# Two plain f blocks per layer instead of three, and an earlier, closer placing of the norm and the token sums in the feed-forward stage

## The chip, the cores and the metric

The kernel runs on one core of one Trainium2 chip. The metric is device time in microseconds (us) of one execution; a smaller number is better. On the core, TensorE (PE) does matmuls into PSUM, VectorE (DVE) and ScalarE (ACT) do elementwise work, GpSimd (POOL) helps in other stages, and SyncE (SP) issues the DMAs.

## The reference, cut to what matters

Two decoder layers of width 1024 on 528 tokens (16 meta tokens and 512 real ones). Each layer is a mixing part and a feed-forward part; the change touches only the second.

```python
hn = rmsnorm(h, ffn_norm_g)
ff = jax.nn.silu(jnp.einsum('bld,df->blf', hn, w_gate)) * jnp.einsum('bld,df->blf', hn, w_up)
return h + jnp.einsum('blf,fd->bld', ff, w_down)          # d = 1024, f = 2816
```

The tensors are float32. The kernel gets that precision from reduced-precision matmuls by splitting each operand into a high and a low part and adding three products: high by high, high weight by low data, low weight by high data.

## The kernel before, in words

The state `h` lies transposed, as eight tiles of 128 rows (k = 0 to 7) by 528 tokens. A layer's feed-forward stage goes over f in 22 blocks of 128 rows, grouped in the six rounds of `ROUNDS` (3, 4, 4, 4, 4, 3 blocks). While the gate and up products of one round run, the down products of the round before are placed between them.

An f block is done in one of two ways.

- A *plain* block (f below `PLAIN`) is two calls of `dense_steps`, one for gate and one for up. Each has 8 steps, one for each k. In layer 0 a step is 6 matmuls of 264 columns (three products, two halves of the tokens); in layer 1, where only the 512 real tokens are wanted, a step is 3 matmuls of 512 columns. So a plain block is 96 matmuls of 264 columns or 48 of 512, recorded at line 217. Its weights are split in pieces of 128x512 by ACT (high part, line 191) and DVE (low part, `wlo`, line 194).
- A `Unit` does gate and up together by a scheme of seven half-size products in place of eight (a Winograd form of a 2 by 2 block product: two weight halves by two halves of the tokens). That is 7 x 4 x 3 = 84 matmuls of 264 columns, or of 256 in layer 1 (line 880). Three of the products take plain halves of the tokens, `xh`/`xl`; the other four take *token sums*, the tiles `th`/`tl`, which `x_forms(0)` to `x_forms(3)` build once per layer: on ACT a scaling (line 841) and a high split (line 142), on DVE four sums of 264 columns (lines 842, 844, 845) and a low split of 1056 columns (line 143). The weights have sums too: `make1` to `make4` build the four weight operands w1 to w4, DVE with four additions (lines 914, 915, 921, 927) and low splits of up to 128x1024 at line 869, ACT with the high splits at line 868. A unit's PE work is in three parts: `head` (24 matmuls, plain token halves, w1), `middle` (36 matmuls; the first of them take w2 and the token sums) and `tail` (24 matmuls). If no down product waits to be placed, a unit's tail stands behind the next unit's head.

Ahead of all this, `start_ffn` scales and splits `h` into `xh` and `xl`. `squares` sums the squares of `h`, and `rstd` turns them into the norm's factor `R`: two matmuls against ones per half (line 290), then a Newton step on DVE (lines 297, 299, 300). `g_done(0)`, the first gate block's evaluation, is held back until `R` exists.

PE's order is the program's order exactly (`tc.manual_schedule`). The other engines' orders are chosen by the scheduler when the kernel is built, and are then fixed: each engine takes its instructions one behind the other and waits on semaphores. Weight loads are issued by SP as soon as a buffer of the ring (`raw`, three deep; `fraw`, two deep) is free.

Of the kernel before, what the change touches and what calls it, by code (L numbers as in the profile page):

```python
# [16 lines left out]
NK = D // 128  # L17
# [7 lines left out]
DFF = 2816  # L25
NF = DFF // 128
ROUNDS = ((0, 3), (3, 7), (7, 11), (11, 15), (15, 19), (19, 22))
PLAIN = 3
HB = NK // 2
EPS = 1e-6  # L30
NBLK = SEQ // 128
# [8 lines left out]
def hybrid_kernel(ctx, tc, x_t, w_in, w_fl, w_out, w_gate, w_up, w_down, vecs, b_fg, rope, decay, mask, ident, out_t):  # L40
# [81 lines left out]
    def sv(t, real, p0=0, p1=128):  # L122
        if real:
            return t[p0:p1, META:T]
        return t[p0:p1, 0:T].rearrange("p (a b) -> p a b", a=2)

    def pv(ps, real, p0=0, p1=128):
        if real:
            return ps[p0:p1, 0, 0:SEQ]
        return ps[p0:p1, :, 0:HALF]  # L130
# [6 lines left out]
    def vcol(c):  # L137
        return vec[:, c:c + 1]


    def split(hi, lo, src, pinned=False):
        pin(nc.scalar.copy(hi, src), pinned)
        pin(nc.vector.tensor_sub(lo, src, hi.bitcast(F32)), pinned)
# [102 lines left out]
    def merge(base, *placed):  # L246

        todo = sorted((p for group in placed for p in group), key=lambda p: p[0])
        out = []
        for i, f in enumerate(base):  # L250
            while todo and todo[0][0] <= i:
                out.append(todo.pop(0)[1])
            out.append(f)
        return out + [f for _, f in todo]
# [11 lines left out]
    def tt(name, dt=F32):  # L266
        tag, bufs = tags[name]
        return tmp.tile([128, T], dt, name=name, tag=tag, bufs=bufs)
# [4 lines left out]
    def fft(tag, dt=F32R, shape=(128, T), bufs=None):  # L273
        return phase["ffn"].tile(list(shape), dt, name=tag, tag=tag, bufs=bufs)

    def col_parts(src, cols, pinned=False):
        c_all = slice(cols[0][0], cols[-1][1])
        sh = tt("sqh", F32R)
        sl = tt("sql", F32R)
        split(sh[:, c_all], sl[:, c_all], src[:, c_all], pinned)  # L280
        return sh, sl

    def col_rstd(parts, n, cols, rname):


        c_all = slice(cols[0][0], cols[-1][1])
        views = [psum_a()[:, 0:c1 - c0] for c0, c1 in cols]
        for i, s in enumerate(parts):
            for v, (c0, c1) in zip(views, cols):
                nc.tensor.matmul(v, ones if s.dtype == F32R else ones.bitcast(F32), s[:, c0:c1], start=(i == 0), stop=(i == len(parts) - 1))  # L290
        with tc.high_priority():
            r = tt(rname)
            a = tt("nwt")
            for v, (c0, c1) in zip(views, cols):
                nc.scalar.activation(r[:, c0:c1], v, AF.Ln, bias=epsc, scale=1.0 / n)
            nc.scalar.activation(r[:, c_all], r[:, c_all], AF.Exp, scale=-0.5)
            nc.vector.tensor_mul(a[:, c_all], r[:, c_all], r[:, c_all])
            for v, (c0, c1) in zip(views, cols):
                nc.vector.scalar_tensor_tensor(a[:, c0:c1], v, n * EPS, a[:, c0:c1], ALU.add, ALU.mult)
            nc.vector.scalar_tensor_tensor(r[:, c_all], a[:, c_all], 3.0 * n, r[:, c_all], ALU.subtract, ALU.mult)  # L300
        return r
# [24 lines left out]
    def squares(st, cols, pinned=False, att=True):  # L326
        c = slice(cols[0][0], cols[-1][1])
        acc = tt("ss")
        for k in range(NK):
            if k == 0:  # L330
                first = nc.scalar.activation(acc[:, c], h[0][:, c], AF.Square)
                if pinned:
                    tc.keep_in_program_order(first)
            else:
                sq = tt("sq")
                more = nc.scalar.activation(sq[:, c], h[k][:, c], AF.Square)
                if pinned:
                    tc.keep_in_program_order(more)
                with ExitStack() if att else tc.high_priority():
                    nc.vector.tensor_add(acc[:, c], acc[:, c], sq[:, c])  # L340
        if pinned:
            st["acc"] = acc
            return
        with ExitStack() if att else tc.high_priority():
            st["parts"] = col_parts(acc, cols)

    def rstd(st, cols, rname="R"):

        st["R"] = col_rstd(st["parts"], D, cols, rname)
# [56 lines left out]
    def silu(t, then=None):  # L406
        nc.scalar.activation(t, t, AF.Silu)
        if then:
            tc.keep_in_program_order(nc.scalar.preload_act_table_set(then))
# [383 lines left out]
    def ffn(l, st, real, last):  # L793
        QC = REAL if real else FULL
# [5 lines left out]
        held = []  # L800

        def two(t):
            return t[:, t0:T].rearrange("p (a b) -> p a b", a=2)
# [4 lines left out]
        def g_done(f):  # L808
            def go(ps):
                sg = tt("sg")  # L810
                if isinstance(ps, list):
                    for v, (c0, c1) in zip(ps, QC):
                        nc.vector.scalar_tensor_tensor(sg[:, c0:c1], v[:, 0:c1 - c0], RSC, st["R"][:, c0:c1],
                                                       ALU.mult, ALU.mult)
                else:
                    nc.vector.scalar_tensor_tensor(sv(sg, real), pv(ps, real), RSC, sv(st["R"], real), ALU.mult, ALU.mult)
                silu(sv(sg, real))
                sgs[f] = sg
            return go
# [14 lines left out]
        def x_forms(k):  # L834
            def go():
                if k == 0:
                    st["t"] = [[fft(f"t{p}{i}", shape=(128, 2, 4, w)) for p in "hl"] for i in range(2)]
                s = fft("S", F32, (128, 6, w), 2)
                a, b = ((h[k][:, c0:c1], h[HB + k][:, c0:c1]) for c0, c1 in HC)
                g0, g1 = vcol(V_FFN + l * NK + k), vcol(V_FFN + l * NK + HB + k)  # L840
                nc.scalar.activation(s[:, 0:2], two(h[k]), AF.Copy, scale=g0)
                nc.vector.tensor_sub(s[:, 2], s[:, 1], s[:, 0])
                for i in range(2):
                    nc.vector.scalar_tensor_tensor(s[:, 3 + i], b[1], g1, s[:, 1 + i], ALU.mult, ALU.subtract)
                nc.vector.scalar_tensor_tensor(s[:, 5], a[1], g1, s[:, 4], ALU.mult, ALU.subtract)
                th, tl = (t[:, k % 2] for t in st["t"][k // 2])
                split(th, tl, s[:, 2:6])
            return go
# [177 lines left out]
        steps = []  # L1026
        tails = []
        fills = []
        for r, (f0, f1) in enumerate(ROUNDS):
            for f in range(f0, f1):  # L1030
                if f < PLAIN:
                    steps += dense_steps(w_gate[l, f], [(0, xs, NK, QC, g_done(f) if f else held.append)], banks=f == 1)
# [10 lines left out]
                if fills:  # L1043
                    p, g0, g1 = fills.pop(0)
# [18 lines left out]
        else:  # L1063
# [149 lines left out]
            places = [(end, after_a)] + [(end + n * (i + 1), f) for i, f in enumerate(  # L1213
                (after_0, after_1, after_2, after_3, after_4, after_5, after_6, after_7))]
            steps += merge(rnd, places)
        for i in range(HB):
            steps.insert(NK + 4 + 9 * i, x_forms(i))
        steps.insert(NK + 4, lambda: g_done(0)(held[0]))
        steps.insert(NK + 4, lambda: rstd(st, QC))
        steps.insert(4, lambda: squares(st, QC, False, False))  # L1220
        return steps

    gf = const.tile([128, NK], F32, name="gf")
    nc.vector.tensor_scalar_mul(gf, vec[:, V_FIN:V_FIN + NK], RSC)
# [1 line left out]
    def layer(l):  # L1226
# [79 lines left out]
        for g in range(2):  # L1306
# [15 lines left out]
                      ret_places(3, 52, 45.5, 47.5, 57.5, 55.5, 58.5, 60, 64.1, 63, 64.2))  # L1322
        plan += [op[3], op[7], op[11], op[15]] + op[16:]
        up = ffn(l, ff, real, real)
        plan += [lambda: enter("ffn"), start_ffn] + up
        return plan
# [78 lines left out]
```

## Time and profile before

| | us |
|---|---|
| median of 3 runs | 1274.46 |
| range of those runs | 1274.37 to 1275.15 |
| the profiled execution, its own time | 1278.19 |
| span of that execution in the trace | 1276.3 |
| feed-forward stage of layer 0 begins (first plain matmul) | about 290 |
| feed-forward stage of layer 1 begins | about 918 |
| granted PE clock, mean over the span | 0.995 |

The profiled execution is 3.7 us over the median of the runs. A page's first block gives each engine's busy time. The chain of waits follows the work that ended last; where it names PE with nothing between, PE never waited there. A row of a timeline gives start, duration, engine, line, operation and, in brackets, idle time ahead of it. A row of the stretches gives a stretch's length, each engine's busy time in it, the granted PE clock and the share of the DMA engines. Two instructions on DVE overlap by some 0.08 us in these records, so the distance from one start to the next is what one costs.

### The profile page before, as it was taken

The page shows a single profiled execution, that of the slowest core. Times are in us where ns is not written, and L with a number is a line of the kernel's source. Part 1 is how long each engine was busy: PE and PEld are TensorE (multiplying, and loading weights), DVE is VectorE, ACT ScalarE, POOL GpSimd, SP SyncE. Part 2 cuts the span into 40 slices and gives each one's busy share as a digit, 9 for nine tenths or more (in the row PEclk, how much of TensorE's full clock was granted, in tenths as well). Part 3 has the DMA queues.
Part 4 walks back from the last instruction along what each step waited for, and adds up shares of the span by engine and source line. Part 5 has one row for each costly group of instructions (what it writes and reads, how often), then busy time and mean ns, then how long its engine had stood idle before and what let it go on. Part 6 is the DMA issues. An engine that isn't in the chain of part 4 may idle for free.

```text
span 1276.3 us, 23615 instructions
## 1 busy us (share of the span) xinstructions
PE 1258.8 (99%) x9271; PEld 1199.9 (94%) x9271; DVE 996.6 (78%) x1843; ACT 688.2 (54%) x1246; POOL 265.2 (21%) x522
## 2 busy tenths in 40 slices
PE   9999999999999999999999999999999999999997
PEld 8899999999999999999998989999789999999996
DVE  7777856779988887887785777567899888888866
ACT  6666545676444444444464665456764444444444
POOL 3355546420000000000025545554100000000000
PEclk9999999999999999999999999999999999999998
DMA  6322232223333333332323232232224333333321
GB/s 216 93 68 84 79 94 72 74 67 112 108 96 100 100 100 100 100 100 83 102 74 100 76 100 84 75 92 67 99 86 129 100 100 100 100 99 101 106 76 67
DMA packets 45680, 120.57 MB, mean 94 GB/s; under 512 B 5360, under 2 KB 12272, under 8 KB 45568
## 3 DMA queue, kind: packets, MB, share of 16 engines
q1 hardware_dynamic: 45136, 118.77, 29.8%
q8 instruction: 73, 1.20, 0.4%
q14 instruction: 39, 0.32, 0.1%
q10 hardware_dynamic: 432, 0.29, 0.1%
HBM read 116.91 MB, written 2.13 MB: 93 GB/s over the span
## 4 chain that ended last, share of the span: by engine, by line
PE 94%; DVE 2%; ACT 1%; DMA 1%; issue 0%; DVEq 0%; ACTq 0%; SPq 0%
PE psd L217 30%; PE psa L880 18%; PE psd L1015 14%; PE psd L880 13%; PE psa L217 5%; PE psa L1015 4%; PE psa L418 2%; PE psa L572 2%; PE psa L507 2%; PE psa L729 1%; PE psa L699 1%; DMA bc<-cdr 1%; PE psa L379 1%; PE psa L290 0%; DMA cdr<-z 0%
## 5 line engine op out<-in xcount | busy, mean ns | idle before, releaser
L194 POOL TENSOR_TENSOR wlo<-raw,whi 128x128 fp32r<-128x128 f32 x504 | 259.9, 551 | 293.5 <-ACT whi L191 293.5
L217 PE MATMUL psd<-xh,whi 128*128 128x264 f32 (+1 forms) x792 | 197.1, 316 | 0.6 <-ACT whi L191 0.6
L217 PE MATMUL psd<-xh,wlo 128*128 128x264 f32 (+1 forms) x792 | 187.7, 305 | 0.0
L217 PE MATMUL psd<-xl,whi 128*128 128x264 f32 (+1 forms) x792 | 187.3, 304 | 0.4 <-DVE xl L320 0.4
L217 PEld LDWEIGHTS psd<-xh,whi 128*128 128x128 f32 x792 | 129.4, 191 | 5.7 <-ACT whi L191 1.3
L217 PEld LDWEIGHTS psd<-xh,wlo 128*128 128x128 f32 x792 | 128.0, 190 | 6.4 <-DVE wlo L194 0.4
L217 PEld LDWEIGHTS psd<-xl,whi 128*128 128x128 f32 x792 | 128.6, 190 | 4.8 <-DVE xl L320 0.8
L191 ACT CAST whi<-raw 128x512 fp32r<-128x512 f32 (+1 forms) x168 | 98.5, 614 | 51.6 <-PE psd L217 38.2
L868 ACT CAST whi<-raw 128x1024 fp32r<-128x1024 f32 (+2 forms) x62 | 54.9, 886 | 51.0 <-PE psd L880 39.5
L868 ACT CAST fwhi<-raw 128x1024 fp32r<-128x1024 f32 (+2 forms) x62 | 55.7, 898 | 46.6 <-PE psd L880 39.2
L1115 POOL TENSOR_TENSOR th<-th,e 128x544 f32<-128x544 f32 x1 | 1.4, 1370 | 359.1 <-DVE e L1135 359.1
L85 POOL MEMSET kl<- 64x528 f32 x2 | 1.1, 534 | 345.4 <-PE psa L880 345.4
L869 DVE TENSOR_TENSOR wlo<-raw,whi 128x1024 fp32r<-128x1024 f32 (+2 forms) x62 | 62.9, 1015 | 12.1 <-ACT whi L868 12.0
L869 DVE TENSOR_TENSOR fwlo<-raw,fwhi 128x1024 fp32r<-128x1024 f32 (+2 forms) x62 | 64.0, 1032 | 9.6 <-ACT fwhi L868 9.5
L880 PE MATMUL psa<-th,whi 128*128 128x264 f32 (+1 forms) x232 | 65.4, 282 | 0.0
L880 PE MATMUL psa<-th,wlo 128*128 128x264 f32 (+1 forms) x232 | 65.4, 282 | 0.0
L880 PE MATMUL psa<-tl,whi 128*128 128x264 f32 (+1 forms) x232 | 65.3, 282 | 0.0
L880 PE MATMUL psa<-th,fwhi 128*128 128x264 f32 (+1 forms) x224 | 63.4, 283 | 0.0
L880 PE MATMUL psa<-tl,fwhi 128*128 128x264 f32 (+1 forms) x224 | 63.3, 283 | 0.0
L880 PE MATMUL psa<-th,fwlo 128*128 128x264 f32 (+1 forms) x224 | 63.2, 282 | 0.0
L527 ACT ACTIVATE probs<-probs,nmax 128x144 f32<-128x144 f32 (+1 forms) x64 | 36.9, 577 | 47.3 <-DVE nmax L514 34.5
L868 ACT CAST fwhi<-S 128x1024 fp32r<-128x1024 f32 x20 | 21.0, 1050 | 69.1 <-PE psa L880 67.1
(340 smaller groups left out, 4053.7 us busy)
## 6 DMA issues: line engine op xcount, KB each, us to landing
raw<-w_in SPq DMA_DIRECT2D x54, 512.0 KB, 3.5
raw<-w_gate SPq DMA_DIRECT2D x44, 512.0 KB, 3.8
fraw<-w_up SPq DMA_DIRECT2D x38, 512.0 KB, 3.5
raw<-w_down SPq DMA_DIRECT2D x64, 256.0 KB, 2.8
raw<-w_out SPq DMA_DIRECT2D x16, 512.0 KB, 3.4
raw<-w_down SPq DMA_DIRECT2D x32, 192.0 KB, 2.5
bc<-cdr SPq DMA_DIRECT2D x16, 264.0 KB, 3.4
raw<-w_up SPq DMA_DIRECT2D x6, 512.0 KB, 3.6
```

What stands on the lines that cost most here:

```text
L191: pin(nc.scalar.copy(hi, job["raw"][:, c0:c1]), pinned)
L194: pin(sub(lo[:, i:i + step], job["raw"][:, c0 + i:c0 + i + step], hi[:, i:i + step].bitcast(F32)), pinned)
L217: nc.tensor.matmul(ps[1][b][:, 0:c1 - c0], w[:, wk, :], x[:, c0:c1], start=(k == 0 and i == 0), stop=(k == n - 1 and i == 2))
L379: nc.tensor.matmul(ps[:, 0:c1 - c0], wf[:, k, :], st["x"][k][part][:, c0:c1], start=(i == 0), stop=(i == 2 * NK - 1))
L418: nc.tensor.transpose(ps[:, 128 * j:128 * j + 128], src[:, o:o + 128], idt)
L507: nc.tensor.matmul(sc[0:nq, 0:c1 - c0], st["q"][s][:, q0:q0 + nq], kk[:, c0:c1], start=(i == 0), stop=(i == 1))
L527: nc.scalar.activation(pr, pr, AF.Exp, bias=nmax[0:nq], scale=-1.0, accum_out=rsum)
L572: nc.tensor.matmul(po[:, c0:SEQ], v[:, j, :], pp[:, j, META + c0:T], start=(j == 0 and i == 0), stop=(j == 4 and i == 1))
L868: nc.scalar.copy(hi, src)
L869: nc.vector.tensor_sub(lo, src, hi.bitcast(F32))
L880: nc.tensor.matmul(bank()[:, 0:b.shape[-1]], a[:, o + k, :], b, start=(fresh and k == 0 and i == 0), stop=(k == n - 1 and i == 2), skip_gr ...
L1015: nc.tensor.matmul(v[:, 0:c1 - c0], a[:, s * n + k, :], b[:, c0:c1], start=(k == 0 and i == 0), stop=(k == n - 1 and i == 2))
```

## The change

`PLAIN` goes from 3 to 2, so f = 2 becomes the first unit of its layer; each layer then has 2 plain blocks and 20 units instead of 3 and 19. The rounds stay. Since round 0 has no down products to place, the tail of unit 2 comes behind the head of unit 3.

The list of places is rewritten with `merge`. Counted in the plain steps, `squares` stays ahead of step 4; `rstd`, `g_done(0)` and `x_forms(0)` move from ahead of step 12 to ahead of step 11; `x_forms(1)` to `(3)` move from ahead of steps 20, 28 and 36 to ahead of steps 16, 21 and 26. There were 48 plain steps before the first unit's head, and there are 32 now.

```diff
-PLAIN = 3
+PLAIN = 2
...
-        for i in range(HB):
-            steps.insert(NK + 4 + 9 * i, x_forms(i))
-        steps.insert(NK + 4, lambda: g_done(0)(held[0]))
-        steps.insert(NK + 4, lambda: rstd(st, QC))
-        steps.insert(4, lambda: squares(st, QC, False, False))
-        return steps
+        return merge(steps, [(4, lambda: squares(st, QC, False, False)), (NK + 3, lambda: rstd(st, QC)),
+                             (NK + 3, lambda: g_done(0)(held[0]))], [(p, x_forms(i)) for i, p in enumerate((11, 16, 21, 26))])
```

PE, layer 0, the up product of f = 0: the difference of the two orders (- before, + now). `sqh` and `sql` are the split sum of squares, `ones` the matrix that sums it.

```order
 L217 MATMUL psd<-xl_4147,whi 128x264 x2
 L217 MATMUL psd<-xh_4146,wlo 128x264 x2
+L290 MATMUL psa<-sqh,ones 128x264 x2
+L290 MATMUL psa<-sql,ones 128x264 x2
 L217 MATMUL psd<-xh_4150,whi 128x264 x2
 L217 MATMUL psd<-xl_4151,whi 128x264 x2
 L217 MATMUL psd<-xh_4150,wlo 128x264 x2
-L290 MATMUL psa<-sqh,ones 128x264 x2
-L290 MATMUL psa<-sql,ones 128x264 x2
 L217 MATMUL psd<-xh_4154,whi 128x264 x2
```

The norm's products moved ahead by one step, six matmuls.

DVE, layer 0, the rows that end with the low split of w2, the first operand that a unit's middle needs. Before the change this is unit 3, behind the three plain blocks:

```order
L825 TENSOR_TENSOR tq<-tq,sg 128x528
L845 SCALAR_TENSOR_TENSOR S<-h_80,vec,S 128x264
L194 TENSOR_TENSOR wlo<-raw,whi 128x512
L143 TENSOR_TENSOR al_4487<-tq,ah_4486 128x528
L914 TENSOR_TENSOR S<-fraw 128x512
L143 TENSOR_TENSOR tl_4306<-S,th_4305 128x1056
L816 SCALAR_TENSOR_TENSOR sg<-psd,R 128x528
L869 TENSOR_TENSOR wlo<-raw,whi 128x1024
L915 TENSOR_TENSOR S<-S,raw 128x512
L921 TENSOR_TENSOR fraw<-raw,fraw 128x512
L927 TENSOR_TENSOR raw<-raw,S 128x512
L869 TENSOR_TENSOR fwlo<-S,fwhi 128x1024
```

The same place with the change, where it is unit 2, behind two plain blocks:

```order
L824 SCALAR_TENSOR_TENSOR tq<-psd,R 128x528
L845 SCALAR_TENSOR_TENSOR S<-h_80,vec,S 128x264
L825 TENSOR_TENSOR tq<-tq,sg 128x528
L914 TENSOR_TENSOR S<-fraw 128x512
L143 TENSOR_TENSOR tl_4300<-S,th_4299 128x1056
L143 TENSOR_TENSOR al_4495<-tq,ah_4494 128x528
L915 TENSOR_TENSOR S<-S,raw 128x512
L921 TENSOR_TENSOR fraw<-raw,fraw 128x512
L927 TENSOR_TENSOR raw<-raw,S 128x512
L869 TENSOR_TENSOR fwlo<-S,fwhi 128x1024
```

The plain split at line 194 and the gate evaluation at line 816, which belong to the third plain block, are gone from this piece; the split of w1 (`wlo<-raw`, 128x1024) stands further up. All the rest is still there. Counted from the low split of the squares (`sql<-ss`, line 143) to this `fwlo<-S` and both included, layer 0 has 51 DVE instructions before the change and 46 with it, layer 1 49 and 44. In both layers the five that are gone are four splits at line 194 and one evaluation at line 816.

## The prediction

> **What bounds the kernel now.** I read the page's busy times first, then who waited for whom, then the two feed-forward openings engine by engine.
>
> ```profile
> PE 1258.8 (99%) x9271; PEld 1199.9 (94%) x9271; DVE 996.6 (78%) x1843; ACT 688.2 (54%) x1246; POOL 265.2 (21%) x522
> ```
>
> PE is the bound: a matmul taken away is worth its time, and a wait put in costs its time. The list of waits says how little PE waits; its longest wait is not in the stage that changes.
>
> ```profile
> PE psa L418 <- DVE vv L484: 1.8, 1, 1.8
> ...
> PE psd L217 <- DVE xl L320: 0.4, 1, 0.4
> ```
>
> The mean of DVE, 78%, hides the stage concerned. The stretches (length, then PE, PEld, DVE, ACT, POOL busy, PE clock, DMA share) run in each layer from the split of the squares to the low split of w2, the first operand of the first unit's middle; the third is a unit with its down products further on.
>
> ```profile
> 295.10:325.07 29.97, 29.97 (x248) 29.82 (x248) 29.93 (x53) 18.29 (x26) 0.00 (x0) 1.00 0.26 84
> 923.53:953.28 29.75, 29.75 (x132) 23.95 (x132) 29.44 (x51) 18.42 (x26) 0.00 (x0) 1.00 0.28 85
> 340.30:354.90 14.60, 14.60 (x122) 14.60 (x122) 12.57 (x20) 6.82 (x11) 0.00 (x0) 1.00 0.30 100
> ```
>
> Here DVE has no idle time: 29.93 of 29.97 us, 29.44 of 29.75. PE and DVE both are full, and PE doesn't wait only because DVE is ahead of it. In the steady units DVE has 2 us of 14.6 to spare. So the question is how far ahead DVE is.
>
> **What PE saves.** The chain of waits is PE alone here (start, duration, line, matmuls).
>
> ```profile
> 308.37 17.36 PE psd L217 x144
> 325.73 1.45 PE psa L880 x12
> ...
> 936.19 16.59 PE psd L217 x72
> 952.77 1.43 PE psa L880 x12
> ```
>
> Layer 0: a plain matmul takes 17.36/144 = 0.1206 us, so the 96 of a plain block take 11.57; the 84 of a unit at 1.45/12 take 10.15: saved 1.4. Layer 1: 48 x 16.59/72 = 11.06, against 84 x 1.43/12 = 10.0: saved 1.1. Together 2.5 us.
>
> **What PE comes to wait for.** The first use of w2's low half on PE, and DVE's rows from the split of the squares to the split that writes it:
>
> ```profile
> 328.70 0.28 PE L880 MATMUL psa<-th,fwlo 128*128 128x264 f32 x1
> 955.69 0.28 PE L880 MATMUL psa<-th,fwlo 128*128 128x256 f32 x1
> ```
>
> ```profile
> 295.10 0.70 DVE L143 TENSOR_TENSOR sql<-ss,sqh 128x528 fp32r<-128x528 f32 x1
> 295.72 1.89 DVE L194 TENSOR_TENSOR wlo<-raw,whi 128x512 fp32r<-128x512 f32 x3
> 297.53 0.42 DVE L842 TENSOR_TENSOR S<-S 128x264 f32<-128x264 f32 x1
> ...
> 320.36 0.70 DVE L816 SCALAR_TENSOR_TENSOR sg<-psd,R 128x528 f32<-128x528 f32 x1
> 320.98 1.22 DVE L869 TENSOR_TENSOR wlo<-raw,whi 128x1024 fp32r<-128x1024 f32 x1
> ...
> 323.92 1.23 DVE L869 TENSOR_TENSOR fwlo<-S,fwhi 128x1024 fp32r<-128x1024 f32 x1
> ...
> 923.53 0.69 DVE L143 TENSOR_TENSOR sql<-ss,sqh 128x512 fp32r<-128x512 f32 x1
> ...
> 952.14 1.23 DVE L869 TENSOR_TENSOR fwlo<-S,fwhi 128x1024 fp32r<-128x1024 f32 x1
> ```
>
> With one plain block fewer, PE reaches this place 11.57 us sooner in layer 0, at 328.70 - 11.57 = 317.13, and 11.06 sooner in layer 1, at 944.63. (The norm's products only change places with six matmuls.) DVE loses five instructions of the stretch: four splits at 297.53 - 295.72 = 1.81 over three, 0.60 each, and one evaluation, 320.98 - 320.36 = 0.62. That is 3.0 us. So the low half of w2 is written at 323.92 + 1.23 - 3.0 = 322.1 in layer 0 and at 952.14 + 1.23 - 3.0 = 950.4 in layer 1. PE waits 5.0 us in layer 0 and 5.7 in layer 1: the lead of 3.6 and 2.3 that it had, plus 3.0, less the 11.57 and 11.06 by which it comes sooner. Together 10.7.
>
> Could the new order or the placing of the sums shorten this? All four sums must be done before the middle, wherever they stand, and DVE's queue, full throughout, holds the same 46 and 44 instructions in any order. New waits inside it can only lengthen it, so 10.7 is near the lower end. The upper end, by rows: DVE waits once in each layer for a cast on ACT (1.06, the row below), 12.8. I take 10.7, since ACT is busy only 18.3 of 30 us.
>
> The wait comes in two pieces, for w2's high half is cast on ACT as soon as the weight sum is there:
>
> ```profile
> 322.83 1.06 ACT L868 CAST fwhi<-S 128x1024 fp32r<-128x1024 f32 x1 [1.03 <-DVE S L915]
> ...
> 951.05 1.05 ACT L868 CAST fwhi<-S 128x1024 fp32r<-128x1024 f32 x1 [1.04 <-DVE S L915]
> ```
>
> 3.0 us sooner it ends at 320.9 and 949.1. PE, there at 316.9 and 944.4 (two matmuls before the places above), stands about 4.0 and 4.7 us, does two matmuls, and stands about another 1.0.
>
> **What the wait does to the clock.** Stretches of 3.41 us, the length of the one spell at half clock inside this trace:
>
> ```profile
> 38.35:41.76 3.41, 2.32 (x20) 2.11 (x19) 1.23 (x7) 0.85 (x4) 3.24 (x8) 1.00 0.46 161
> 680.06:683.47 3.41, 1.02 (x7) 0.50 (x6) 1.99 (x9) 2.18 (x8) 1.70 (x4) 1.00 0.13 49
> 683.47:686.88 3.41, 3.41 (x11) 2.93 (x12) 2.82 (x10) 0.72 (x2) 0.00 (x0) 0.50 0.44 150
> 1263.74:1267.15 3.41, 2.08 (x12) 1.36 (x11) 2.95 (x8) 1.78 (x6) 0.00 (x0) 1.00 0.47 163
> 1267.15:1270.56 3.41, 1.56 (x4) 0.77 (x3) 2.10 (x5) 2.42 (x7) 0.00 (x0) 0.50 0.47 163
> ```
>
> All five lie on one grid of 3.41 us. After a piece of the grid with PE busy 1.02 or 2.08 us the clock was halved; after one with 2.32 it was not. A fully busy piece gave the clock back. A wait of 5 us leaves at least 2.5 idle in some piece, wherever the grid falls, hence at most 0.9 busy: the clock is halved in both layers, before PE starts again or as it does. It comes back after the next fully busy piece, so between 3.4 and 6.8 us of work run at half clock and half of that is lost: 1.7 to 3.4 us. The grid's place is open, so I take the middle, 2.5, twice: 5.0. The lower bound is 0, if the two matmuls between the waits count for more than they seem to.
>
> [...]
>
> **Unit 2's result.** Its tail now stands between unit 3's head and middle, and the first down product takes its result as the third of three blocks. In before, a unit's evaluation ran from its first DVE row to its last:
>
> ```profile
> 338.82 0.70 DVE L956 TENSOR_TENSOR sg<-psd,e 128x528 f32<-128x528 f32 x1
> 344.88 0.71 DVE L143 TENSOR_TENSOR al<-tq,ah 128x528 fp32r<-128x528 f32 x1
> ...
> 965.65 0.68 DVE L956 TENSOR_TENSOR sg<-psd,e 128x512 f32<-128x512 f32 x1
> 972.34 0.69 DVE L143 TENSOR_TENSOR al<-tq,ah 128x512 fp32r<-128x512 f32 x1 [0.69 <-ACT ah L142]
> ```
>
> 6.8 and 7.4 us. Meanwhile PE has unit 3's middle (36 matmuls, 4.4) and two blocks of the down product (12, or 6 wide ones, 1.4), some 5.9. The price is 0 to 1.5 us a layer. I take 0.3 for both together, near the low end, since at half clock PE leaves DVE time.
>
> **What costs nothing.** The norm's products come 0.7 us sooner, at 298.3 and 926.6; their operand was written at 295.8 and 924.2 (the `sql` rows above).
>
> ```profile
> 299.00 0.41 PE L290 MATMUL psa<-sqh,ones 128*128 128x264 f32 x2
> ...
> 927.28 0.40 PE L290 MATMUL psa<-sqh,ones 128*128 128x512 f32 x1
> 289.71 0.90 SPq L904 DMA_DIRECT2D fraw<-w_up  x2
> 297.07 0.33 SPq L158 DMA_DIRECT2D raw<-w_gate  x1
> ```
>
> SP loads the same bytes. The first two units' up weights are issued at 289.71, and unit 2's gate weights take the place of the plain gate load at 297.07, 20 us ahead of their use. POOL has nothing in these stretches.
>
> **The sum.** -2.5 + 10.7 + 5.0 + 0.3 = +13.5 us. The profiled execution would go from 1278.19 to 1291.7; it stands 3.7 over the median of the runs, and 1274.46 + 13.5 = 1288.0. A measurement of this kernel can tell about 0.2%, 2.5 us, from no change.
>
> **The rivals.**
> - *DVE keeps pace* (the other side): PE saves 2.5 and waits for nothing: 1272.0. It needs w2's low half by 317.1 and 944.6, 5.0 and 5.7 us sooner than the rows give. For it speaks only that DVE was 3.6 and 2.3 us ahead; against it stands a queue without idle time. The change is faster only if the two waits together are under 2.5.
> - *PE waits, but the clock stays*: 1274.46 - 2.5 + 10.7 + 0.3 = 1283.0. For it: two matmuls break the wait, and the spell in the trace followed a piece with 2.4 idle, not a wait of this form. Against it: 2.08 us busy did not suffice. With the clock lost in one layer alone it is 1285.5. [...]
> - *Half a wait*: some of DVE's rows ahead of w2 turn out to have been slack, and about 5.4 of the 10.7 stay: 1277.4.
> - *Not the change it says*: the matmuls don't fall, or saving and waits cancel: 1274.5. The order shows the plain block gone, so little speaks for it.
>
> **How the numbers follow.** Waits and half clock in both layers 0.60 (own range 1285.5 to 1290.9, from the clock's 3.4 to 6.8 and the unit's 0 to 1.5), clock kept in one layer or both 0.25, half a wait 0.07, nothing 0.03, DVE keeps pace 0.05. The range from 1281.5 to 1290.5 holds the first two cases but their outer ends, some 8 in 10. Faster 0.05, same 0.03, slower 0.92.
>
> **What would show it.** In the changed trace PE should wait at line 880 for `fwhi` (ACT), then `fwlo` (DVE), some 5 us in each layer, DVE without idle time up to that split, and a spell of 3.4 us or more at half clock should stand behind each wait. Line 217's `psd<-xh,whi` should fall from 792 to 744. If the low half of w2 is there before PE, the step on DVE is wrong; if PE waits at full clock afterwards, the step on the clock.

## The result, and the profile after

| | before | with the change |
|---|---|---|
| median, us | 1274.81 | 1288.6 |
| range, us | 1274.37 to 1276.35 | 1288.21 to 1289.65 |
| runs | 4 | 4 |
| the profiled execution's own time, us | 1278.19 | 1288.41 |
| its span, us | 1276.3 | 1286.6 |
| granted PE clock, mean | 0.995 | 0.993 |

The change makes the kernel slower: the ratio is 1.0102, with a 95% interval of 1.009 to 1.0114, or +13.8 us between the medians. The forecast was 1288.0.

The page of the changed kernel first: busy times, the chain of waits by engine, and the group of plain matmuls of which the change removes some.

```profile
PE 1258.2 (98%) x9295; PEld 1199.9 (93%) x9295; DVE 1006.4 (78%) x1857; ACT 692.5 (54%) x1252; POOL 265.9 (21%) x522
...
PE 87%; DVE 8%; ACT 3%; DMA 1%; issue 1%; ACTq 0%; DVEq 0%; SPq 0%
...
L217 PE MATMUL psd<-xh,whi 128*128 128x264 f32 (+1 forms) x744 | 182.8, 314 | 1.2 <-ACT whi L191 1.2
```

The chain and the same group in the kernel before:

```profile
PE 94%; DVE 2%; ACT 1%; DMA 1%; issue 0%; DVEq 0%; ACTq 0%; SPq 0%
...
L217 PE MATMUL psd<-xh,whi 128*128 128x264 f32 (+1 forms) x792 | 197.1, 316 | 0.6 <-ACT whi L191 0.6
```

The plain matmuls went from 792 to 744 for this group. PE's busy time fell by only 0.6 us; a part of its work now runs at half clock (0.50 granted in the pieces below). DVE's share of busy time is what it was, 78%; what changed is that 8% of the chain that ended last now goes through DVE, where it was 2%.

The list of waits of PE (engine, tile, line, what it waited for: total us, times, longest) has four rows that stand nowhere in the list of before:

```profile
PE psa L880 <- ACT fwhi L868: 8.0, 2, 4.2
...
PE psa L880 <- DVE fwlo L869: 1.2, 2, 0.8
...
PE psd L1015 <- DVE al L143: 0.9, 1, 0.9
PE psa L1015 <- DVE al L143: 0.9, 1, 0.9
```

PE's timeline shows the places: the first unit's middle, and the down product that takes that unit's result, in layer 0 and in layer 1.

```profile
319.40 0.59 PE L880 MATMUL psa<-th,fwhi 128*128 128x264 f32 x1 [3.87 <-ACT fwhi L868]
320.67 0.59 PE L880 MATMUL psa<-th,fwlo 128*128 128x264 f32 x1 [0.46 <-DVE fwlo L869]
340.04 0.51 PE L1015 MATMUL psa<-al,fwhi 128*128 128x264 f32 x2 [0.87 <-DVE al L143]
...
952.67 0.39 PE L880 MATMUL psa<-th,fwhi 128*128 128x256 f32 x1 [4.17 <-ACT fwhi L868]
953.94 0.58 PE L880 MATMUL psa<-th,fwlo 128*128 128x256 f32 x1 [0.76 <-DVE fwlo L869]
972.12 0.50 PE L1015 MATMUL psd<-al,fwhi 128*128 128x512 f32 x1 [0.92 <-DVE al L143]
```

Without the waits the matmul with `fwlo` would have begun two matmuls of 0.12 us after PE came to the place, at 319.40 - 3.87 + 0.24 = 315.77 in layer 0 and at 952.67 - 4.17 + 0.24 = 948.74 in layer 1. So PE lost 4.9 and 5.2 us there.

The stretches (length, then PE, PEld, DVE, ACT and POOL busy, PE clock, DMA share): the first runs from the split of the squares to the low split of w2 in layer 0, the others are pieces of the clock's grid.

```profile
293.59:320.55 26.96, 22.75 (x182) 22.09 (x181) 26.86 (x48) 16.47 (x23) 0.00 (x0) 0.97 0.19 55
...
315.28:318.69 3.41, 0.26 (x3) 0.04 (x1) 3.41 (x5) 1.40 (x3) 0.00 (x0) 1.00 0.00 0
318.69:322.10 3.41, 2.24 (x8) 1.93 (x9) 3.41 (x5) 3.08 (x4) 0.00 (x0) 0.50 0.02 5
322.10:325.52 3.42, 3.42 (x18) 3.42 (x17) 3.38 (x6) 0.38 (x1) 0.00 (x0) 0.50 0.72 186
325.52:328.90 3.38, 3.38 (x30) 3.38 (x30) 2.59 (x4) 1.61 (x3) 0.00 (x0) 1.00 0.31 122
950.16:953.57 3.41, 0.51 (x2) 0.30 (x2) 3.41 (x6) 2.00 (x3) 0.00 (x0) 1.00 0.00 0
953.57:956.98 3.41, 3.04 (x14) 3.05 (x15) 3.41 (x5) 1.84 (x3) 0.00 (x0) 0.50 0.24 44
```

DVE is busy 26.86 of 26.96 us: it never waits, PE does. Behind each wait stands a spell at half clock, 6.8 us in layer 0 (318.69 to 325.52) and 3.4 in layer 1 (953.57 to 956.98). PE works in them from 320.67 and from 953.94 on, so half of 4.85 and of 3.04 us is lost: 2.4 and 1.5.

### The profile page after: what moved, and what is told of

The parts are those of the page before. It is cut to its first block, busy times and chain, and to the rows that moved or that the text cites. A ratio compares the mean times of both kernels' runs of the same rounds, so it can differ in the third digit from the quotient of the medians.

```text
span 1286.6 us, 23683 instructions
## 1 busy us (share of the span) xinstructions
PE 1258.2 (98%) x9295; PEld 1199.9 (93%) x9295; DVE 1006.4 (78%) x1857; ACT 692.5 (54%) x1252; POOL 265.9 (21%) x522
## 4 chain that ended last, share of the span: by engine, by line
PE 87%; DVE 8%; ACT 3%; DMA 1%; issue 1%; ACTq 0%; DVEq 0%; SPq 0%
PE psd L217 25%; PE psa L880 19%; PE psd L1015 14%; PE psd L880 13%; PE psa L1015 4%; PE psa L217 4%; PE psa L418 2%; PE psa L572 2%; PE psa L507 1%; PE psa L729 1%; PE psa L699 1%; DVE tl L143 1%; PE psa L379 1%; DMA bc<-cdr 1%; DVE S L844 0%
## 5 line engine op out<-in xcount | busy, mean ns | idle before, releaser
L217 PE MATMUL psd<-xh,whi 128*128 128x264 f32 (+1 forms) x744 | 182.8, 314 | 1.2 <-ACT whi L191 1.2
L217 PE MATMUL psd<-xl,whi 128*128 128x264 f32 (+1 forms) x744 | 173.4, 301 | 0.6 <-DVE xl L320 0.6
L217 PE MATMUL psd<-xh,wlo 128*128 128x264 f32 (+1 forms) x744 | 173.8, 302 | 0.0
L217 PEld LDWEIGHTS psd<-xh,whi 128*128 128x128 f32 x744 | 120.1, 189 | 5.6 <-ACT whi L191 2.0
L217 PEld LDWEIGHTS psd<-xh,wlo 128*128 128x128 f32 x744 | 118.9, 188 | 5.6 <-DVE wlo L194 0.4
L217 PEld LDWEIGHTS psd<-xl,whi 128*128 128x128 f32 x744 | 119.3, 188 | 4.5 <-DVE xl L320 1.2
L191 ACT CAST whi<-raw 128x512 fp32r<-128x512 f32 (+1 forms) x160 | 93.6, 613 | 50.9 <-PE psd L217 38.6
L880 PE MATMUL psa<-th,whi 128*128 128x264 f32 (+1 forms) x248 | 69.9, 282 | 0.0
L880 PE MATMUL psa<-th,wlo 128*128 128x264 f32 (+1 forms) x248 | 69.9, 282 | 0.0
L946 ACT COPY e<-psa 128x264 f32<-128x264 f32 (+1 forms) x120 | 45.1, 376 | 37.0 <-PE psa L880 33.0
```

Of the source, the lines that this page charges most:

```text
L191: pin(nc.scalar.copy(hi, job["raw"][:, c0:c1]), pinned)
L217: nc.tensor.matmul(ps[1][b][:, 0:c1 - c0], w[:, wk, :], x[:, c0:c1], start=(k == 0 and i == 0), stop=(k == n - 1 and i == 2))
L880: nc.tensor.matmul(bank()[:, 0:b.shape[-1]], a[:, o + k, :], b, start=(fresh and k == 0 and i == 0), stop=(k == n - 1 and i == 2), skip_gr ...
L946: nc.scalar.copy(self.t["e"][:, i], self.t["x"][:, 0:w])
```

## The experiments

Each ratio is to runs of the kernel before on the same chip; the medians of those were 1275.17 us (for the places, the plain block, the filler, and GpSimd in the changed kernel), 1275.74 (the extra work and the orders) and 1275.22 (the rest). The theory: DVE's queue up to the low split of w2 is what PE waits for, and the half clock follows from the wait. The main rivals: the new places of the sums do the harm; or the wait has a cause besides DVE's work.

### The places alone, and the plain block alone

Places as in the change, three plain blocks as before:

```diff
-PLAIN = 2
+PLAIN = 3
```

> Three plain blocks as before, only the new places of norm and token sums (11, 16, 21, 26). Theory (VectorE is full in the opening of the feed-forward stage, and PE waits only when its order comes to the first unit before VectorE has w2): VectorE's work up to w2's low split is 29.9 us in layer 0 and 30.3 in layer 1 by the rows of the trace, PE needs it after 33.3 and 32.0, so no wait: 1274.8, the same as before within 1.5. Rival (the closer places, not the missing plain block, cost the time): about 1288.

Measured: 1276.38 us, ratio 1.0007 (0.9998 to 1.0015): no difference. Its list of waits has no row of line 880 or 1015, and the granted clock is 1.00 in every piece of both stages. The places do no harm while three plain blocks stand ahead.

The other half, two plain blocks with the sums placed as before:

```diff
-        return merge(steps, [..., (NK + 3, ...), (NK + 3, ...)], [... enumerate((11, 16, 21, 26))])
+        return merge(steps, [..., (NK + 4, ...), (NK + 4, ...)], [... enumerate((12, 20, 28, 36))])
```

> Two plain blocks, the norm and the sums at the old places 12, 20, 28, 36. Theory: VectorE ends the last token sum, now behind w2's split, 29.8 us (layer 0) and 29.0 (layer 1) after the split of the squares; PE comes to that operand 23.1 and 22.2 after it, so waits of 6.7 and 6.8 in place of about 5 each: 3 us slower than the change as made, about 1292. Rival (the places are what costs the time): near 1272 to 1275. Second rival (places don't matter, only the plain block does): 1288.6.

Measured: 1293.31 us, ratio 1.0143 (1.013 to 1.0157). Its waits of PE, and a spell at half clock in each layer:

```profile
PE psa L880 <- ACT th L142: 7.5, 2, 4.4
...
PE psa L880 <- DVE tl L143: 1.6, 2, 0.8
...
PE psa L880 <- DVE fwlo L869: 1.5, 2, 0.8
PE psa L880 <- ACT fwhi L868: 1.4, 1, 1.4
```

```profile
319.44:329.68 10.24, 5.67 (x24) 5.37 (x25) 8.77 (x14) 3.02 (x4) 0.00 (x0) 0.50 0.31 102
954.32:964.56 10.24, 6.34 (x27) 5.75 (x28) 9.06 (x14) 3.29 (x5) 0.00 (x0) 0.50 0.32 102
```

The removed block carries the whole loss: the new places alone cost nothing, and the missing block alone costs 18 us. The waits come to 12.0 us here and the half clock lasts three pieces of the grid; the closer places take back 0.0041 of the time, 5 us. They do so because the wait then ends on w2 alone and not on w2 and, later, on the last sums.

### The same extra work, in the kernel before and in the changed one

The first of the four sums of each `x_forms` (line 842) is computed three times, which the rows price at 8 x 0.34 = 2.7 us of DVE in each layer.

```diff
-                nc.vector.tensor_sub(s[:, 2], s[:, 1], s[:, 0])
+                for _ in range(3):
+                    nc.vector.tensor_sub(s[:, 2], s[:, 1], s[:, 0])
```

> The kernel before, with line 842's subtraction done three times in each token sum: 8 x 0.34 = 2.7 us more work on VectorE in each layer, ahead of w2. Theory (VectorE was 3.6 and 2.3 us ahead of PE there, and only that lead is used up): waits of 0 in layer 0 and about 0.5 in layer 1, 1275 to 1276.5. Rival (VectorE's work in this stretch is on the path already): 5.4 slower, 1280.

> The changed kernel with the same extra work. VectorE's work up to w2's low split becomes 28.4 us in layer 0 and 28.3 in layer 1 by the rows (26.9 and 26.1 in the change; one addition of the weights falls behind it), so each wait should grow by as much, 1.5 + 2.2 = 3.7: about 1292, and a little more where the half clock moves with it (0 to 3). Rival (the wait is on something else than VectorE's queue): 1288.6.

Measured: 1276.39 us and 1.0009 (0.9998 to 1.0019) in the kernel before, where one wait of 0.8 us for `fwlo` appears, in layer 1; 1292.77 us and 1.0127 (1.0114 to 1.014) with the change, 0.0025 or 3.2 us over the change alone. In the latter (line 881 is the old 880, 870 the old 869):

```profile
PE psa L881 <- ACT fwhi L869: 9.2, 2, 4.6
...
PE psa L881 <- DVE wlo L870: 1.6, 2, 1.1
PE psa L881 <- DVE fwlo L870: 1.5, 2, 1.0
```

So the lead of 3.6 and 2.3 us that was read from the trace before was real and could be spent; in the changed kernel nothing of it is left. That the changed kernel lost 3.2 us and not twice 2.7 was expected in the main (3.7), since one addition of the weights falls behind w2's split there.

### The clock by itself

Sixteen matmuls of 512 columns, whose result nobody reads, stand ahead of unit 2's middle, so that PE works while it would wait.

```diff
+        def filler():
+            idle = psum_a()
+            for _ in range(16):
+                nc.tensor.matmul(idle, ones, st["x"][0][0][:, META:T], start=True, stop=True)
...
+                if f == PLAIN:
+                    steps.append(filler)
```

> The change, and in each layer 16 more matmuls of 512 columns into a bank that nobody reads, between the head and the middle of the first unit, where PE stands still. They take 16 x 0.23 = 3.7 us of a wait of about 5 and keep the clock up; no idle spell over 1.3 us stays. Theory (half clock costs 1.7 to 3.4 us a layer): 3.4 to 6.8 faster than the change, about 1284, with no spell at half clock in the feed-forward stage. Rival (the clock costs nothing, only the wait does): 1288.6. Other rival (the waits are not where the theory has them): 7.4 slower, 1296.

Measured: 1285.06 us, ratio 1.0078 (1.0065 to 1.0091), 0.0024 or 3.1 us below the change. No stretch of the two stages is at half clock: the granted clock is 1.00 in every piece. So the half clock costs some 3 us, and keeping PE busy with nothing gains them back; the trace of the change gave 3.9. What stays is the wait itself, now as filler, and the late result at line 1015 (two waits of 0.9, as in the change).

### DVE's work taken away

The cleanest test of the theory: some low splits are left out, both in the changed kernel and in the one before. One of the places in the edit:

```diff
...
-            nc.scalar.copy(hi, src)
-            nc.vector.tensor_sub(lo, src, hi.bitcast(F32))
+            nc.scalar.copy(hi, src)
+            if lo is not hi:
+                nc.vector.tensor_sub(lo, src, hi.bitcast(F32))
...
```

> The change with some of DVE's work of the stage left out, and nothing else: no low part is made of the up weights of f = 0, of both weights of f = 1, of w1 of unit 2, nor of the first two token sums; PE does the same number of matmuls of the same shapes, with the high part read in place of the low one (the output loses that precision). In the changed trace's rows that takes 6 x 0.60 + 1.13 + 2 x 1.17 = 7.1 us from DVE's queue ahead of w2's low half in layer 0, where PE waited 4.9. If DVE's work is the whole cause, no wait and no half clock is left at the first unit's middle, and the time is that of before less the matmuls, 1274.8 - 2.5 = 1272.3, or up to 1274.1 if unit 2's result is still 0.9 late in each layer. Rival: something else in the stage (the casts on ACT, the weights' arrival, the order on PE) holds the middle up for part of the time: 1278 or more, with a wait at line 888 for another engine.

> The control for the run before: the same low parts are left out of the kernel before (there the weights of f = 2 too). If the lead that DVE had before the change was slack, nothing moves: 1274 to 1275.5. If PE were held up by DVE somewhere else in the stage too, it falls below 1273.

Measured: 1278.34 us and 1.0025 (1.0015 to 1.0035) with the change; 1275.78 us and 0.9999 (0.999 to 1.0008) in the kernel before. The control came as expected. In the changed kernel half of the expectation held: no wait is left at the first unit's middle, and the granted clock is 1.00 there in both layers. But it is 3 us slower than before where 1 to 3 us faster was expected. That is the time of the rival (1278 or more), but not for the rival's reason, for no engine holds the middle up. Its waits of PE show why (line 1027 is the old 1015):

```profile
PE psa L1027 <- ACT ah L142: 2.3, 1, 2.3
...
PE psd L1027 <- DVE al L143: 0.9, 1, 0.9
...
PE psa L1027 <- DVE al L143: 0.8, 1, 0.8
...
PE psd L1027 <- ACT ah L142: 0.4, 1, 0.4
```

```profile
328.66:332.07 3.41, 2.28 (x19) 2.06 (x17) 3.00 (x5) 1.23 (x3) 0.00 (x0) 1.00 0.61 207
332.07:335.48 3.41, 1.46 (x9) 1.25 (x10) 3.25 (x7) 0.63 (x1) 0.00 (x0) 1.00 0.02 5
335.48:338.89 3.41, 3.41 (x18) 3.41 (x17) 0.78 (x3) 1.05 (x1) 0.00 (x0) 0.50 0.00 0
```

PE, no longer held up, comes to the down product sooner than unit 2's result: 4.4 us of waits, and in layer 0 a spell of 3.41 us at half clock, 1.7 lost. The sum -2.5 + 4.4 + 1.7 = +3.6 stands against the measured 3.1. So a second gap stood behind the first: only unit 3's middle and two blocks of the down product lie between unit 2's tail and the use of its result. (The order of DVE was chosen anew for this kernel, so the rows ahead of that result are not those of the change less the splits.)

### Low splits on GpSimd

The low splits of the plain blocks, all but those of the gate of f = 0, go from DVE to GpSimd in pieces of 128x128: in the changed kernel six splits a layer, 6 x 0.60 = 3.6 us of DVE; then the same in the kernel before.

```diff
-... g_done(f) if f else held.append)], banks=f == 1)
+... g_done(f) if f else held.append)], pool=f > 0, banks=f == 1)
-... dense_steps(w_up[l, f], [(0, xs, NK, QC, u_done(f))])
+... dense_steps(w_up[l, f], [(0, xs, NK, QC, u_done(f))], pool=True)
```

> The change, but the low splits of the plain up 0, gate 1 and up 1 go to GpSimd, which has nothing to do there. Theory: VectorE's work up to w2's low split falls from 26.9 to 22.1 us in layer 0 and from 26.1 to 21.9 in layer 1, PE needs it after 22.0 and 21.1: waits of 0 and 1, clock kept, the saving of 2.5 comes through, less up to 1.8 for unit 2's result: 1272.5 to 1275. Rival (GpSimd is too slow or slows VectorE): PE waits for GpSimd at the plain blocks, 1277 or more.

> The kernel before with the low splits of its plain blocks (all but the gate of f = 0) on GpSimd, in pieces of 128x128. No time is at stake: PE has a lead of 3.6 and 2.3 us. If GpSimd at work lengthens DVE's instructions whatever the kernel, the subtraction of 264 columns at line 842, the split of the squares and of h beside it read about 0.69, 0.96 and 0.85 instead of 0.42, 0.70 and 0.75, and the time stays at 1274 to 1277. If those rows were an effect of the changed order, they read as in before.

Measured: 1289.52 us and 1.0116 (1.0103 to 1.013) with the change, 1295.69 us and 1.0155 (1.0141 to 1.0169) in the kernel before. Both times were missed, by 14 us and more. Line 842's subtraction on DVE, as a group (durations in ns: least, median, largest), in the kernel before and then in that kernel with the splits on GpSimd:

```profile
L842 DVE TENSOR_TENSOR S<-S x8: 418/424/429, 297.5 to 938.4; 128x264 f32<-128x264 f32 x4, 128x256 f32<-128x256 f32 x4
```

```profile
L842 DVE TENSOR_TENSOR S<-S x8: 411/546/692, 295.2 to 943.3; 128x264 f32<-128x264 f32 x4, 128x256 f32<-128x256 f32 x4
```

In the changed kernel with those splits the median is 0.679 us. While GpSimd works, such an instruction takes up to 0.69 us in place of 0.42, so part of what was taken from DVE comes back as longer instructions. In the changed kernel's DVE rows the low split of w2 starts 25.8 us behind that of the squares (319.39 and 293.59), with the splits on GpSimd 24.1 (319.50 and 295.37): 1.7 gained of 3.6. So the waits at the middle shrank, to 1.9 and 2.5 us, but PE waited 0.9 and 0.5 for w1's split ahead of them and 2.3, 0.8 and 0.9 for unit 2's result, longer than in the change, as in the kernel with less work on DVE. The rows of the kernel before with the splits on GpSimd show the other effect, here on GpSimd, SP, DVE and PE in turn:

```profile
304.39 12.53 POOL L194 TENSOR_TENSOR wlo<-raw,whi 128x128 fp32r<-128x128 f32 x16 [3.90 <-ACT whi L191]
321.31 4.57 POOL L194 TENSOR_TENSOR wlo<-raw,whi 128x128 fp32r<-128x128 f32 x8 [4.39 <-ACT whi L191]
```

```profile
325.91 0.33 SPq L904 DMA_DIRECT2D raw<-w_gate  x1
```

```profile
329.40 0.69 DVE L915 TENSOR_TENSOR S<-S,raw 128x512 f32<-128x512 f32 x1 [5.50 <-DMA raw<-w_gate]
```

```profile
332.50 0.59 PE L880 MATMUL psa<-xh,wlo 128*128 128x264 f32 x1 [4.58 <-DVE wlo L869]
```

GpSimd's last split ends at 321.31 + 4.57 = 325.88 and frees a `raw` buffer; only then, at 325.91, is the gate weight issued into it (SP's four waits of line 904 for GpSimd come to 20.9 us in this run, the longest 6.5); in the kernel before that load went out at 318.09. DVE idles 5.5 us for it, and PE then waits 4.6 for w1's split. That the splits cost time even where DVE had a lead is due to the weight ring, not to DVE's queue alone.

### Order in place of work

DVE's order is changed: first w2's rows of unit 2 are given priority in the change.

```diff
-                nc.vector.tensor_add(s[:, HB:NK], b[:, 0:HB], b[:, HB:NK])
-                nc.vector.tensor_sub(s[:, 0:HB], s[:, HB:NK], a[:, 0:HB])
-                splits(hi, lo, s)
+                with tc.high_priority() if self.f == PLAIN else ExitStack():
+                    nc.vector.tensor_add(s[:, HB:NK], b[:, 0:HB], b[:, HB:NK])
+                    nc.vector.tensor_sub(s[:, 0:HB], s[:, HB:NK], a[:, 0:HB])
+                    splits(hi, lo, s)
```

> The change, with the additions and splits of unit 2's w2 given high priority, so that VectorE does them ahead of a plain block's last evaluation and of the other weight additions. VectorE reaches w2's low split 23.3 and 23.2 us after the split of the squares, the last token sum 25.1 and 24.3; PE wants the first after 22.0 and 21.1, the second 1.1 later. Theory: waits of 2.0 and 2.1 instead of about 5 each, half clock perhaps still, unit 2's result 0.9 late in each layer as in the change: 1278 to 1283. Rival (the wait is on ACT's casts or the loads): 1288.6.

Measured: 1292.19 us, ratio 1.0122 (1.0108 to 1.0135): missed, and no better than the change. At the middle the waits did shrink, to 1.9 us in layer 0 and 2.1 in layer 1. The list of waits (line 1016 is the old 1015) and the pieces of the grid in layer 0 show where they went:

```profile
PE psd L1016 <- ACT ah L142: 2.4, 1, 2.4
PE psa L1016 <- ACT ah L142: 2.3, 1, 2.3
PE psa L880 <- DVE fwlo L869: 2.1, 2, 1.1
```

```profile
315.87:319.28 3.41, 1.90 (x12) 1.47 (x12) 3.41 (x5) 2.42 (x3) 0.00 (x0) 1.00 0.02 5
319.28:322.69 3.41, 3.41 (x16) 3.18 (x15) 3.41 (x5) 2.05 (x3) 0.00 (x0) 0.50 0.00 0
```

The work that DVE had passed over still had to be done ahead of unit 2's result: its evaluation ended at 337.89 us in layer 0, as in the change, and PE, less held up at the middle, waited for it there instead. Short waits at the middle (1.5 us within a piece of 3.41) halved the clock all the same. The two stages have four spells at half clock here (0.50 in the pieces from 319.28, 339.76, 954.16 and 974.64).

Then PE's order as well: unit 3's head ahead of unit 2's middle, to give DVE 24 matmuls more, and unit 3's tail ahead of the first down product. The split of unit 3's w1 is given priority too; the lines of PE's order are these:

```diff
...
-                u = Unit(f)
-                steps += u.head()
+                u = heads.pop() if heads else Unit(f)
+                if f == PLAIN:
+                    heads.append(Unit(f + 1))
+                if f != PLAIN + 1:
+                    steps += u.head()
+                if f == PLAIN:
+                    steps += heads[0].head()
...
+                    if f == PLAIN + 1:
+                        u.last()
+                        steps += u.tail()
                     j = down_job(p, g0, g1)
...
```

> As the run with priority, and PE does unit 3's head (24 matmuls that need no token sum) ahead of unit 2's middle, and unit 3's tail ahead of the first down product. That gives VectorE 2.9 us at one more split of 1.13. w2 is ready 24.4 us after the split of the squares and wanted after 24.9 (layer 0); layer 1 about 24.4 against 23.9. Theory: waits under 1 us, full clock, and the saving of 2.5 comes through: 1272.5 to 1274.5, about equal to the kernel before or a little faster. Rival (a unit more costs time elsewhere too): 1276 or more.

Measured: 1281.02 us, ratio 1.0028 (1.0016 to 1.004). That is 0.0094 or 12 us below the kernel with the priority alone and some 9 below the change, but still above the kernel before. With more of PE's work ahead of the first down product, the wait for unit 2's result is down to 0.4 us (line 1017 is the old 1015). What is left is a new wait, since a tail now follows its middle directly and needs the bank that ACT must copy first, and one spell at half clock in the two stages:

```profile
PE psa L880 <- ACT e L948: 2.9, 4, 1.1
...
PE psa L1017 <- DVE al L143: 0.4, 1, 0.4
```

No version with two plain blocks that was run beats the kernel before.

## Why the prediction was right, point by point

The time, 1288.0 against 1288.6, and the likeliest case came as forecast. Term by term, us for both layers:

| term | predicted | in the trace |
|---|---|---|
| PE's saving | -2.5 | matmuls gone as counted |
| wait for w2's low half | 5.0 + 5.7 = 10.7 | 4.9 + 5.2 = 10.1 |
| half clock | 2.5 + 2.5 = 5.0 | 2.4 + 1.5 = 3.9 |
| unit 2's result late | 0.3 | 0.9 + 0.9 = 1.8 |
| sum | +13.5 | +13.3 |

The mechanism came as forecast. That the sum came so near is in part luck: the wait was taken 0.6 us too long, the clock 1.1 too dear and unit 2's result 1.5 too cheap, and the three errors cancel. The forecast's own range for its likeliest case, 1285.5 to 1290.9, does not follow from its terms: with 3.4 to 6.8 for the clock and 0 to 1.5 in each layer for unit 2's result they give 1286.1 to 1292.5.

- *What bounds the kernel.* That DVE, at 78% on average, was full in this stage and that its lead was what counted held: 2.7 us more work in each layer cost nothing that could be told from noise in the kernel before, and 3.2 us in all in the changed one; with 7.1 us of work taken away the waits at the middle were gone.
- *The wait.* It came in the two pieces named, `fwhi` from ACT (3.87 and 4.17, predicted 4.0 and 4.7) and `fwlo` from DVE. The places of the sums, costed at nothing, cost nothing by themselves; the forecast's claim that the queue's length counts "in any order" is true of this change only, since at the old places the last sum stands behind w2's split and other rows, and two plain blocks are some 5 us worse again.
- *The clock.* It was halved in both layers (0.50 granted), and the filler showed that this is a cost of its own (3.1 us). The term was taken too high: in layer 1 the piece with 3.04 us busy was enough to bring the clock back, and I had counted on a fully busy one. The forecast read its five stretches as if PE's busy time in a piece decided; that is not borne out, as the last section shows, though the step did not hang on it. Nor did PE have to stand idle for a whole piece: with the priority alone, the piece 315.87 to 319.28 had PE busy 1.90 of 3.41 us, and the clock was halved behind it.
- *Unit 2's result.* This is the mis-sized term: 0.3 taken for both layers, 1.8 found, inside the stated 0 to 1.5 in each. The rows before, 6.8 against 5.9 us, gave 0.9 for layer 0, which is what came. The reason for taking less, that PE at half clock leaves DVE time, was wrong: the half clock was over at 325.52, 8 us before unit 2's evaluation began on DVE at 333.75. DVE's order decides instead. In the changed kernel's DVE rows the w1 split of a later unit and an addition of unit 3's evaluation stand ahead of `al`:

```profile
337.47 0.42 DVE L964 TENSOR_TENSOR tq<-e,tq 128x264 f32<-128x264 f32 x1
337.81 1.22 DVE L869 TENSOR_TENSOR fwlo<-raw,fwhi 128x1024 fp32r<-128x1024 f32 x1
338.94 0.42 DVE L949 TENSOR_TENSOR e<-psd,e 128x264 f32<-128x264 f32 x1
339.29 0.70 DVE L143 TENSOR_TENSOR al<-tq,ah 128x528 fp32r<-128x528 f32 x1
```

  Its evaluation ends at 337.47 + 0.42 = 337.89, and ACT's high part `ah` begins at once; `al` is put off to 339.29 by a split of 1.22 us, and PE waits 0.9.
- *The rival on the other side.* "DVE keeps pace" was given 1272.0. The kernel with DVE's work taken away shows that this price was wrong as well: with no wait at the middle the time is 1278.3, since the wait at unit 2's result grows to 4.4 us and halves the clock once. The late result was partly hidden by the wait ahead of it.
- *The sum against the spans.* The right column takes the -2.5 over from the forecast, so the stages are worth measuring whole, on PE's timeline. From its first plain matmul to the first matmul behind it, layer 0's stage takes 357.8 us before (290.02 to 647.81) and 365.5 with the change (288.52 to 653.99). From its first plain matmul to its last down matmul, layer 1's takes 328.7 (918.08 to 1246.74) and 335.2 (921.97 to 1257.20). That is 7.7 and 6.6, together 14.2 us more. The two profiled spans differ by only 10.3, because the execution before lost time elsewhere: 2.3 us between the two stages, where its trace has the spell at half clock at 683.47 and the changed kernel's has none, and 1.5 ahead of the first stage. So most of its 3.7 us over the median lies outside the stages, and putting the sum on the median was right.

Not settled: where the 0.9 us lie by which layer 0's stage grew more than its terms add up to (7.7 against 6.8; in layer 1 it is 6.6 against 6.5), and what decides the scheduler's choice ahead of `al`.

## What to carry to other kernels

Before taking work from the busiest engine, ask how far ahead the second engine is at the place where the work goes, in that stage and not on average: a gain of 2.5 us on PE moved PE 11 us forward in each layer past a lead of 2 to 4. The wait cost more than its length here, since it halved the clock (0.50 granted): work that nobody reads, put into it, won back 3.1 us, though not the wait. And when one wait is removed, look for the next use of a result behind it: here it was hidden, and took back 4.4 us and a spell at half clock.

## What the hardware showed that was not expected

- A piece of the clock's grid of 3.41 us with PE busy 1.46, 1.90 or 0.26 us was followed by half clock, one with 2.28 us was not. No whole idle piece is needed, but PE's busy time alone does not decide it either: in the changed kernel's trace the pieces 687.33 to 690.74 and 946.74 to 950.16, with PE busy 1.83 and 1.76 us, were followed by full clock. What else counts stays open. Behind a wait, a piece with 2.24 us busy at half clock left it halved and one with 3.04 brought it back.
- GpSimd at work lengthens some of DVE's instructions. In the kernel before with the splits on GpSimd, a subtraction of two tiles in SBUF at 128x264 (line 842) took 0.69 us at 295.20 in place of 0.42. Beside the same splits, line 825 (two inputs in SBUF) took 0.97 us at 309.52 in place of 0.70, while line 824 (one in PSUM) kept 0.69 at 307.13. In these rows the added time was about the same whatever the size: 0.27 us at 264 and at 528 columns, 0.25 for the split of 128x1056 at line 143 (1.51 at 315.09 in place of 1.26). Not every row grew so, with GpSimd at work all the same: line 845 read 0.58 at 299.58 in place of 0.48, line 842 kept 0.42 at 306.17, and the split at 307.74 kept 1.24 us. What decides it, these rows do not show. GpSimd's own pieces read 12.53/16 = 0.78 and 4.57/8 = 0.57 us there, and 4.45/8 = 0.56 in the changed kernel with the splits, beside a DVE without idle time; the time added to a DVE instruction is less than one such piece takes.
